# A decoder layer on one core: mixer products in another order, weight tiles in another place, x written later

## The chip, the cores and the metric

The kernel runs on one core of one Trainium2 chip. The metric is the device time of one execution in microseconds (us), and less is better. Before the change the median of three runs is 936.56 us (935.53 to 938.85).

A core has a matrix engine (TensorE, PE in the profile, with its weight loads as PEld), a vector engine (DVE), a scalar engine (ACT), GpSimd (POOL) and a sync engine (SP) that here only issues DMAs. Each engine works through its own queue of instructions in order and waits on semaphores for the others. Matmul results go to PSUM, eight banks of 128 x 512 float32 here; everything else lives in SBUF.

## The reference

One layer on x of 512 tokens by 1024 columns, all in float32: a half-step SwiGLU FFN, a token mixer, another half-step FFN, each between RMS norms.

```python
x = x + 0.5 * rms_norm(swiglu_ffn(rms_norm(x, norm_pre[0]), ffn1_w_in, ffn1_w_out), norm_post[0])
mixed = token_mixer(rms_norm(x, norm_pre[1]), w_mix_in, conv_w, ..., w_mix_out)
x = x + rms_norm(mixed, norm_post[1])
x = x + 0.5 * rms_norm(swiglu_ffn(rms_norm(x, norm_pre[2]), ffn2_w_in, ffn2_w_out), norm_post[2])
```

The mixer projects the normed x with w_mix_in into nine groups of columns. Four of 512 columns feed HGRN2 (query hq, forget hf, value hi, gate hgate), the others an mLSTM (query and key through a causal convolution, value mv, output gate mo, and eight gate rows). Both are recurrences over chunks of tokens.

```python
hg_o = rms_norm(hgrn2_chunkwise(silu(hq), 1 - forget, hi, log(forget))) * silu(hgate)
ml_o = rms_norm(mlstm_chunkwise(q, k, mv, log_i, log_f)) * sigmoid(mo)
mixed = concatenate([hg_o, ml_o]) @ w_mix_out
```

## The kernel before

**Precision.** TensorE multiplies in a rounded float32 form (fp32r). Each operand is split into a rounded part and the rest, and a product takes three matmuls (high by high, high by low, low by high). Weights come by DMA into `raw` tiles; ACT rounds them into the tile `w` (L289), or with a scale per row (L294), and DVE makes the rest (L291, or L297). `split` does both for one item of weights. Activations are split the same way into `xq0` to `xq3`, the four quarters of the transposed x (by half of the tokens and half of the columns): after 128 x 128 transposes on PE (L359), ACT rounds (L365) and DVE makes the rest (L366).

**Where the weight tiles lie.** All `w` tiles are cut out of one long SBUF tile of four places. `lie` chooses a place and an offset in it, from a list for each kind of item: `"any"` prefers offset 0, `"mix"` prefers 16 elements (64 bytes) less, `"out"` 80 elements less. With the offset 0 a tile's address is 480 mod 512 bytes, with -16 it is 416. In `split` a mixer item is of kind "mix" if its tile is 256 (`QUARTER`) or 512 columns wide, except those of w_mix_out that are "out".

**The two units.** The products for hgate ("hg") and mo ("mo"), each 512 tokens by 512 columns by 1024, are made from seven quarter products instead of eight. `job_unit` runs p1 to p7 in the order of `UNIT`; each has 24 matmuls of 256 columns (L1181) on one weight tile and one quarter, or a sum of quarters, of x. Results accumulate in PSUM banks: `bank["b6"]` holds sums into which p6 and then p3 accumulate; p2 runs on top of p1's bank, p4 on top of p5's; p7 has its own. After a product the combinations are made: p1's bank is copied (L1191, ACT), p5 has it subtracted and goes to b6 (L1170, DVE), p6's bank is copied by ACT (L1198) and p7's added by DVE. `put` is called for each finished quarter of the result: for hg an ACT silu (`job_kept`), for mo an ACT sigmoid (L1896) and a DVE multiply into y (L1898), both in `gate_mo`. p3 writes into bank b6 and so waits until p6 has been taken out of it.

**Sums of quarters.** p3, p5, p6 and p7 take differences and sums of x's quarters. `x_sums` queues eight DVE instructions (L1138, 128 x 1024 each), of which four add the two parts of a quarter and four combine them; two casts on ACT and a DVE subtraction each (`sum_parts`, L1161 and L1162) round and split them. They write over the tiles `xs0` to `xs3`, which hold x itself. So x is first written to DRAM, by four DMAs of 512 KB on SP (`spill`, L1839), and read back before the mixer's output is added.

**The order of the work.** The program is emitted once, in order; the queue of an engine is the order in which its instructions were emitted. `self.jobs` holds generators of PE work, and `fill`, `chunks` and `until` take steps of them between the steps of the recurrences; `self.extra` holds small pieces such as the x sums that are taken along. `until(name)` runs jobs until that name is in `self.got`. A planner of due times issues loads and splits ahead of their use. `behind(i)` has what follows scheduled only after the instruction i; `self.loaded` is the last weight load that was issued.

The mixer goes in this order: FFN 1's last tiles, the spills and x sums, the gate weights and forget gates (`hf`), then `hgrn_levels` for the first pair of heads (on DVE and ACT the tiles q, qe, qd, kk, ek, el, with L1478, L1481, L1429, L1439, L1471, L1472; on PE the scores L1490 in pairs of 16 matmuls), filled up with the projections of hq and the convolution (L544), then the second pair, hi and mv, the states, the mLSTM scores, the hg unit, the mLSTM values, the mo unit within the HGRN values. In the HGRN values DVE reduces the squares of a chunk (L1769), POOL makes the power (L350, L351), DVE scales into y (L1775); ACT makes the squares (L1766). After `until("mo")` sixteen transposes of y's HGRN half (`to_t`, L359) lead to `mix_out0`, whose matmuls are L193 to L195 (512 columns wide); it transposes the other half in its second part. At the same time POOL and SP build sums of weight quarters for FFN 2 in DRAM (`f2sums`, accumulating DMAs of POOL at L902).

Of the kernel before, what the change touches and what calls it, by code (L numbers as in the profile page):

```python
# [10 lines left out]
AF = mybir.ActivationFunctionType  # L11
ALU = mybir.AluOpType
# [6 lines left out]
NT = T // P  # L19
# [7 lines left out]
QUARTER = 256  # L27
# [1 line left out]
NH = 4  # L29
W = 512  # L30
HQ, HF, HI, HG, MQ, MV, MO, MG = 0, 512, 1024, 1536, 2048, 2560, 3072, 3584
UNIT = ("p1", "p5", "p7", "p2", "p6", "p4", "p3")
UNITS = (HG, MO)
LEVELS = (1, 64, 32, 16, 8, 4, 2)
TINY = 1e-37
# [85 lines left out]
class Layer:  # L121
# [144 lines left out]
    def split(self):  # L266

        nc = self.nc
        it = self.items.popleft()
        raw = self.raw[it.key]  # L270
        _, a, b = raw.shape
        if it.dst:
            w = it.dst()
        else:
            if self.wt is None:
                self.wt = self.wp.tile([P, 2 * D * WBUF + FRONT + PAD], F32R, name="w")
            if not self.slot and it.key[0] != "mix":
                self.free = deque(FREE2 if it.key[0] == "f2" else FREE)
            n, o = self.lie("out" if it.key[1] == "out" else "mix" if it.key[0] == "mix" and b >= QUARTER else "any")
            self.free.remove(n)  # L280
            w = self.wt[:, o : o + 2 * D].rearrange("p (b k t) -> p b k t", b=2, k=a)
            self.slot[id(w)] = n, o, w
        hi, lo = self.both(w)
        if it.sums:
            raw, hi, lo = (self.flat(v)[:, QUARTER:] for v in (raw, hi, lo))
        self.ready.append((w, it.dst is not None))
        rows = it.rows
        if rows is None:
            nc.scalar.copy(hi, raw)  # L289
            yield  # L290
            self.low = nc.vector.tensor_tensor(lo, raw, hi.bitcast(F32), op=ALU.subtract)  # L291
        else:
            for j in range(a):
                nc.scalar.activation(hi[:, j], raw[:, j], AF.Copy, scale=rows[:, j : j + 1])  # L294
            yield
            for j in range(a):
                nc.vector.scalar_tensor_tensor(  # L297
                    lo[:, j], raw[:, j], rows[:, j : j + 1], hi[:, j].bitcast(F32), op0=ALU.mult, op1=ALU.subtract
                )
        with self.behind(*self.hold):  # L300
            for out, other in it.adds:
                o, c = self.raw[out], self.raw[other]

                late = out[1] >= (HEAD if out[0] == "f1" else 1)
                added = (nc.vector if late else nc.gpsimd).tensor_tensor(o, o, c, op=ALU.add)  # L305
                if not late:
                    self.pooled.append(added)
        self.load_due(self.done)
        self.done += 1
        yield  # L310
# [51 lines left out]
    def two(self, dst, i, src):  # L362

        v = slice((i % 2) * P, (i % 2 + 1) * P)
        self.nc.scalar.copy(dst[:, 0, :, v], src)  # L365
        self.low = self.nc.vector.tensor_tensor(dst[:, 1, :, v], src, dst[:, 0, :, v].bitcast(F32), op=ALU.subtract)  # L366
# [798 lines left out]
    def job_unit(self, name, put, keep):  # L1165

        if name == "hg":
            self.sum_parts("p6", "p3")
        nc, bank = self.nc, {"b6": self.whole}
        tt = lambda out, a, b, op: nc.vector.tensor_tensor(out, a, b, op=op)  # L1170
        two = lambda t: t.rearrange("p (c f) -> p c f", c=2)
        into = {"p2": "p1", "p4": "p5", "p6": "b6", "p3": "b6"}
        for p in UNIT:
            w, x = self.pull(), self.unit_x[p]
            if p not in into:
                bank[p] = self.ps()
            ps, n = bank[into.get(p, p)], 0
            for a, b in ((0, 0), (0, 1), (1, 0)):
                for c in range(2):
                    for k in range(KH):  # L1180
                        nc.tensor.matmul(  # L1181
                            ps[:, QUARTER * c : QUARTER * (c + 1)], x[a][:, k, P * c : P * (c + 1)], w[:, b, k, :],
                            start=p not in into and n == 0, stop=(a, k) == (1, KH - 1), skip_group_check=True,
                        )
                        n += 1
                        if n % 6 == 0 and n < 24:
                            yield
            self.drop(w)
            if p == "p1":
                first = keep(1, 0)  # L1190
                nc.scalar.copy(first, two(ps))  # L1191
            elif p == "p5":
                tt(two(bank["b6"]), two(ps), first, ALU.subtract)
            elif p == "p2":
                put(0, 0, two(ps))
            elif p == "p6":
                rest = keep(1, 1)
                nc.scalar.copy(rest, two(ps))  # L1198
                tt(rest, two(bank["p7"]), rest, ALU.add)
            elif p == "p4":  # L1200
                last = keep(1, 0, two(ps))
                tt(last, two(ps), rest, ALU.subtract)
                put(1, 1, rest)
                put(1, 0, last)
            elif p == "p3":
                put(0, 1, two(ps))
                self.got.add(name)
            yield

    def job_kept(self, name, place, func):  # L1210

        def put(u, v, src):
            if u == 0:
                self.nc.scalar.activation(place(u, v), src, func)
            elif v == 0:
                for v in range(2):
                    self.nc.scalar.activation(place(1, v), place(1, v), func)

        return self.job_unit(name, put, lambda u, v, ps=None: place(u, v))
# [605 lines left out]
    def mixer(self):  # L1825
        nc, tc = self.nc, self.tc
        self.got, self.jobs = set(), deque()
        self.sums_due(("f2",), AHEAD, EARLY["f2"])
        with tc.tile_pool(name="ma", bufs=1) as ma:
# [5 lines left out]
            self.kdt = ma.tile([P, NH, 3 * P], F32, name="kdt")  # L1835
            self.S = self.kdt.rearrange("p h (c v) -> p h c v", v=P)
            self.eend = ma.tile([P, 16], F32, name="eend")
            for i in range(NT):
                nc.sync.dma_start(self.spill[i], self.xs[i])  # L1839
            self.x_sums()  # L1840
            with tc.tile_pool(name="mb", bufs=1) as mb:
                self.mb = mb
                kes = [mb.tile([P, 2, T], F32, name=f"ke{n}") for n in range(2)]
                self.q = [mb.tile([P, 2, T], F32, tag="q", bufs=2, name=f"q{p}") for p in range(2)]
                qps = {}
                for n in range(NH):
                    self.jobs.append(self.job_f(f"hq{n}", lambda ps, n=n: qps.__setitem__(n, ps)))
                for n in range(4):
                    self.jobs.append(self.job_f(f"conv{n}", lambda ps, n=n: self.conv(n, ps)))
                self.jobs.append(self.job_rows())  # L1850
                self.jobs.append(self.job_t("hi", lambda i, ps: nc.scalar.copy(self.vh[:, i].rearrange("p h v -> p (h v)"), ps)))
                self.jobs.append(
                    self.job_t("mv", lambda i, ps: nc.scalar.copy(self.vm[:, i, :, :P], ps.rearrange("p (h v) -> p h v", h=NH)))
                )

                with tc.issue_after(self.pow.ins):
                    self.gate_weights(ma, mb)
                self.forget_gates(mb)
                for ke in kes:
                    nc.scalar.copy(ke, self.kk[0])  # L1860
                with tc.issue_after(self.pow.ins):
                    nc.gpsimd.memset(self.sT, 0.0)
                    self.masks(ma, mb)
                    nc.gpsimd.memset(self.vm[:, :, :, P : P + 1], 1.0)
                self.until("hq3")
                for n in range(NH):
                    nc.scalar.activation(self.q[n // 2][:, n % 2], qps[n], AF.Silu)
                self.hgrn_levels(0, kes, FILL[0])
                self.until("rows")
                nc.scalar.activation(self.qk, self.qk, AF.Silu)  # L1870
                self.hgrn_levels(1, kes, FILL[1], self.gate_rows(ma))
            with tc.tile_pool(name="mc", bufs=1) as mc:
# [7 lines left out]
                self.chunks(self.mlstm_values, FILL[2])  # L1880
                self.until("hg")
                self.chunks(self.hgrn_values, FILL[3])
                self.until("mo")
                for i in range(NT):
                    self.to_t(i, self.y[:, i], (0,))
                self.new_x()
                for i in range(NT):
                    nc.sync.dma_start(self.xs[i], self.spill[i])
# [2 lines left out]
    def keep_mo(self, u, v, ps=None):  # L1891
        return self.st("mo").rearrange("p (c f) -> p c f", c=2) if ps is None else ps

    def gate_mo(self, u, v, g):
        nc = self.nc
        nc.scalar.activation(g, g, AF.Sigmoid)  # L1896
        y = self.y[:, 2 * u : 2 * u + 2, W + QUARTER * v : W + QUARTER * (v + 1)]
        nc.vector.tensor_tensor(y, y, g, op=ALU.mult)  # L1898

# [128 lines left out]
```

## Time and profile before

| | |
|---|---|
| median of three runs | 936.56 us |
| profiled execution | 935.1 us, its span 933.4 |
| granted TensorE clock, mean | 0.997 |
| busy: PE, DVE, ACT, POOL | 919.5, 789.1, 537.7, 215.3 us |
| matmuls | 7567, of which 336 at L1181 |
| DMA | 161.19 MB, queue q1 49.1% and q0 14.7% of 16 engines' span |

The trace is one profiled execution. A line of a timeline gives the start in us from the start of the span, the busy time, engine, line, operation, out<-in, shape and count of a run of like instructions, and in brackets the idle time before it with what ended it. A line of a table of windows gives the length, then the busy time of PE, PEld, DVE, ACT and POOL with counts, the granted TensorE clock, the share of the DMA engines' time and GB/s. A line of the waits gives the waiting engine and line, what it waited for, and the total, the number and the longest of these waits. The busy time of a matmul overlaps that of the next, so what one costs is read from start to start. A waiting time can be read as lost only on the engine that sets the end; that is mostly PE, which is busy 99% of the span.

### The profile page before, as it was taken

The numbers are of one execution on the slowest core, as the hardware profiler recorded it, in microseconds if no ns is written. First come the engines' busy times: TensorE is split into PE (matmuls) and PEld (weight loads), VectorE is DVE, ScalarE is ACT, GpSimd is POOL, SyncE is SP. The second block draws the span as 40 slices with busy tenths as digits, with TensorE's granted clock in tenths as the row PEclk, the third lists the DMA queues.
The fourth block names the chain that finished last, engine by engine and source line by source line (L and its number), as shares of the span: only waits on it lengthen the run. The fifth ranks groups of instructions, "written<-read, shape, count | busy, mean of one in ns | idle before, by whom it ended". The sixth has DMA issues, their size and how long they took to land.

```text
span 933.4 us, 18752 instructions
## 1 busy us (share of the span) xinstructions
PE 919.5 (99%) x7567; PEld 892.1 (96%) x7567; DVE 789.1 (85%) x1016; ACT 537.7 (58%) x773; POOL 215.3 (23%) x280
## 2 busy tenths in 40 slices
PE   9999999999999999999999989999999999999997
PEld 7999999999999999998889978899999999999997
DVE  6899988889887879698868674799898989998886
ACT  7645545557566466956536454595454545756661
POOL 3565112132122047452331310304000000011002
PEclk9999999999999999999999999999999999999999
DMA  9869869887897834797854454452453445278542
GB/s 314 224 161 245 208 176 206 203 181 184 237 265 237 260 131 121 150 183 193 174 115 117 141 173 132 138 159 67 138 159 115 136 122 171 82 218 262 168 153 91
DMA packets 131025, 161.19 MB, mean 173 GB/s; under 512 B 8405, under 2 KB 103673, under 8 KB 130938
## 3 DMA queue, kind: packets, MB, share of 16 engines
q1 hardware_dynamic: 110490, 140.59, 49.1%
q0 software_dynamic: 20160, 18.88, 14.7%
q8 instruction: 59, 0.97, 0.4%
q10 hardware_dynamic: 288, 0.52, 0.2%
q14 instruction: 28, 0.23, 0.1%
HBM read 155.77 MB, written 41.94 MB: 212 GB/s over the span
## 4 chain that ended last, share of the span: by engine, by line
PE 56%; DVE 3%; issue 2%; POOL 1%; ACT 1%; DVEq 0%; POOLq 0%; ACTq 0%
PE ps L615 22%; PE ps L970 8%; PE ps L544 6%; PE ps L962 4%; PE ps L193 3%; PE ps L195 3%; PE ps L194 3%; PE ps L1490 2%; PE ps L1181 2%; PE ps L554 1%; POOL col L351 1%; DVE w L291 1%; PE ps L359 1%; ACT w L294 0%; PE ps L1583 0%
## 5 line engine op out<-in xcount | busy, mean ns | idle before, releaser
L289 ACT CAST w<-raw 128x1024 fp32r<-128x1024 f32 x252 | 257.6, 1028 | 179.3 <-PE ps L615 91.4
L291 DVE TENSOR_TENSOR w<-raw,w 128x1024 fp32r<-128x1024 f32 x252 | 306.3, 1220 | 18.8 <-ACT w L289 17.7
L615 PE MATMUL ps<-xq,w 128*128 128x256 f32 x2016 | 237.2, 277 | 0.0
L615 PEld LDWEIGHTS ps<-xq,w 128*128 128x128 f32 x2016 | 232.9, 188 | 0.0
L615 PE MATMUL ps<-sq,w 128*128 128x256 f32 x1512 | 177.9, 276 | 0.3
L615 PEld LDWEIGHTS ps<-sq,w 128*128 128x128 f32 x1512 | 174.2, 188 | 0.9 <-ACT ps L666 0.9
L305 DVE TENSOR_TENSOR raw<-raw,raw 128x1024 f32<-128x1024 f32 x72 | 89.8, 1251 | 7.9 <-DMA raw<-in_ffn_w_in_dram 6.3
L970 PE MATMUL ps<-w,hs 128*128 128x256 f32 x672 | 81.3, 276 | 0.0
L962 PE MATMUL ps<-w,hs 128*128 128x256 f32 x672 | 79.2, 276 | 0.0
L970 PEld LDWEIGHTS ps<-w,hs 128*128 128x128 f32 x672 | 78.5, 188 | 0.2 <-DVE y L486 0.2
L962 PEld LDWEIGHTS ps<-w,hs 128*128 128x128 f32 x672 | 77.5, 188 | 0.0
L902 POOL DMA_DIRECT2D f2sums<-in_ffn_w_out_dram x15 | 19.5, 1426 | 177.8 <-DMA f2sums<-in_ffn_w_out_dram 176.9
L544 PE MATMUL ps<-xq,w 128*128 128x256 f32 x480 | 55.7, 277 | 0.0
L544 PEld LDWEIGHTS ps<-xq,w 128*128 128x128 f32 x480 | 54.9, 188 | 0.5 <-issue 0.5
L193 PE MATMUL ps<-w,xq 128*128 128x512 f32 x128 | 51.2, 403 | 2.0 <-ACT xq L365 1.9
L194 PE MATMUL ps<-w,xq 128*128 128x512 f32 x128 | 49.9, 391 | 0.0
L195 PE MATMUL ps<-w,xq 128*128 128x512 f32 x128 | 49.6, 391 | 0.1
L834 ACT CAST hs<-hf 128x1024 fp32r<-128x1024 f32 x32 | 33.7, 1053 | 27.5 <-PE ps L970 19.8
L902 POOL DMA_DIRECT2D f2sums<-f2sums x30 | 25.2, 879 | 87.2 <-DMA f2sums<-in_ffn_w_out_dram 50.5
L835 DVE TENSOR_TENSOR hs<-hf,hs 128x1024 fp32r<-128x1024 f32 x32 | 39.1, 1221 | 6.6 <-ACT hs L834 6.1
L305 POOL TENSOR_TENSOR raw<-raw,raw 128x1024 f32<-128x1024 f32 x12 | 31.6, 2640 | 41.0 <-DVE w L291 39.6
L448 ACT ACTIVATE junk<-ps 128x256 f32<-128x256 f32 (+1 forms) x40 | 17.1, 428 | 40.7 <-DVE ps L927 20.1
(287 smaller groups left out, 1355.6 us busy)
## 6 DMA issues: line engine op xcount, KB each, us to landing
raw<-in_ffn_w_in_dram SPq DMA_DIRECT2D x98, 512.0 KB, 4.6
raw<-in_ffn_w_out_dram SPq DMA_DIRECT2D x44, 512.0 KB, 5.5
raw<-in_w_mix_in_dram SPq DMA_DIRECT2D x26, 512.0 KB, 4.1
raw<-f2sums SPq DMA_DIRECT2D x15, 512.0 KB, 3.3
raw<-f1sums SPq DMA_DIRECT2D x13, 512.0 KB, 5.9
raw<-unit SPq DMA_DIRECT2D x8, 512.0 KB, 4.3
raw<-in_w_mix_out_dram SPq DMA_DIRECT2D x8, 512.0 KB, 4.1
f2sums<-in_ffn_w_out_dram SPq DMA_DIRECT2D x30, 128.0 KB, 5.7
```

What stands on the lines that cost most here:

```text
L193: mm(ps, sh, mh, start=start, stop=False, **kw)
L194: mm(ps, sh, ml, start=False, stop=False, **kw)
L195: mm(ps, sl, mh, start=False, stop=stop, **kw)
L289: nc.scalar.copy(hi, raw)
L291: self.low = nc.vector.tensor_tensor(lo, raw, hi.bitcast(F32), op=ALU.subtract)
L305: added = (nc.vector if late else nc.gpsimd).tensor_tensor(o, o, c, op=ALU.add)
L544: mm(ps[:, u0:u1], w[:, a, k, :], self.xop(k, b, u0, u1), start=k + n + m == 0, stop=k == ND - 1 and n == 2, skip_group_check=True,)
L615: self.nc.tensor.matmul(ps[:, c], wb[b][:, k, v], left[d][:, k, :], start=first and a + n + k == 0, stop=n == 2 and k == KH - 1, skip_grou ...
L835: self.nc.vector.tensor_tensor(lo, src, hi.bitcast(F32), op=ALU.subtract)
L902: nc.gpsimd.dma_start(to[:, a:b], v, accum_op=ALU.add)
L962: mm(out, a[kk][:, i * P : (i + 1) * P], w[:, b, kk, QUARTER * v : QUARTER * (v + 1)], start=begin and c == kk == n == 0, stop=kk == 1 and ...
L970: mm(ps[:, QUARTER * c : QUARTER * (c + 1)], A[a][:, c], B[b], start=begin and c == n == 0, stop=n == 2, skip_group_check=True,)
```

## The change

- `UNIT` changes from p1, p5, p7, p2, p6, p4, p3 to p1, p5, p7, p6, p2, p3, p4, and the weights are loaded in that order.
- In `job_unit` ACT copies p7's bank (instead of p6's), as soon as p7 is done, and DVE adds p6's bank to the copy. That quarter is put at once, its sigmoid for mo going into p7's bank (`spare`). p3 comes before p4 and adds the name "mo3" to `got`.
- In the mixer, `until("mo3")` leads to the sixteen transposes, and `until("mo")`, with p4, comes after them.
- In `split` a mixer tile is of kind "mix" only if it is 512 columns wide; the 256-wide ones are "any".
- The four spill DMAs and `x_sums()` move from the start of the mixer to after the forget gates, behind the last load issued there. On DVE the first of the eight adds then stands between two levels of the first pair of heads, after an L291, and the other seven spread over the next 28 instructions; on ACT the two casts L1161 come between the casts and exponentials of the same levels.

On DVE the add of p6's bank in the mo unit stands behind the fourth L1769 of the HGRN values and ahead of two L297 and the fourth chunk's L1775.

```diff
-UNIT = ("p1", "p5", "p7", "p2", "p6", "p4", "p3")
+UNIT = ("p1", "p5", "p7", "p6", "p2", "p3", "p4")
...
-            n, o = self.lie("out" if it.key[1] == "out" else "mix" if it.key[0] == "mix" and b >= QUARTER else "any")
+            n, o = self.lie("out" if it.key[1] == "out" else "mix" if it.key[0] == "mix" and b == 512 else "any")
...
+            elif p == "p7":
+                rest = keep(1, 1)
+                nc.scalar.copy(rest, two(ps))
+            elif p == "p6":
+                tt(rest, two(ps), rest, ALU.add)
+                put(1, 1, rest, two(bank["p7"]))
             elif p == "p2":
                 put(0, 0, two(ps))
-            elif p == "p6":
-                rest = keep(1, 1)
-                nc.scalar.copy(rest, two(ps))
-                tt(rest, two(bank["p7"]), rest, ALU.add)
+            elif p == "p3":
+                put(0, 1, two(ps))
+                self.got.add(name + "3")
             elif p == "p4":
                 last = keep(1, 0, two(ps))
                 tt(last, two(ps), rest, ALU.subtract)
-                put(1, 1, rest)
                 put(1, 0, last)
-            elif p == "p3":
-                put(0, 1, two(ps))
                 self.got.add(name)
             yield
...
-        def put(u, v, src):
+        def put(u, v, src, spare=None):
...
-            for i in range(NT):
-                nc.sync.dma_start(self.spill[i], self.xs[i])
-            self.x_sums()
             with tc.tile_pool(name="mb", bufs=1) as mb:
...
                 self.forget_gates(mb)
+                with self.behind(self.loaded):
+                    for i in range(NT):
+                        nc.sync.dma_start(self.spill[i], self.xs[i])
+                self.x_sums()
                 for ke in kes:
                     nc.scalar.copy(ke, self.kk[0])
...
-                self.until("mo")
+                self.until("mo3")
                 for i in range(NT):
                     self.to_t(i, self.y[:, i], (0,))
+                self.until("mo")
                 self.new_x()
...
-    def gate_mo(self, u, v, g):
-        nc = self.nc
-        nc.scalar.activation(g, g, AF.Sigmoid)
+    def gate_mo(self, u, v, src, spare=None):
+        nc = self.nc
+        g = src if spare is None else spare
+        nc.scalar.activation(g, src, AF.Sigmoid)
         y = self.y[:, 2 * u : 2 * u + 2, W + QUARTER * v : W + QUARTER * (v + 1)]
         nc.vector.tensor_tensor(y, y, g, op=ALU.mult)
```

## The prediction

> **What bounds the kernel now.** I read the busy table of the page first, then the waits of TensorE, then timelines of PE, DVE, ACT and POOL around each edited place.
>
> ```profile
> PE 919.5 (99%) x7567; PEld 892.1 (96%) x7567; DVE 789.1 (85%) x1016; ACT 537.7 (58%) x773; POOL 215.3 (23%) x280
> ```
> ```profile
> PE ps L1181 <- ACT mo L1198: 2.4, 1, 2.4
> PE ps L193 <- ACT xq L365: 1.9, 1, 1.9
> PE ps L189 <- POOL ident masks.py:199: 1.6, 1, 1.6
> PE ps L554 <- DVE w L291: 0.8, 1, 0.8
> PE ps L1181 <- DVE y L1808: 0.2, 1, 0.2
> ```
> TensorE is busy all but 14 us. So an edit can save only a cheaper matmul or one of these waits, of which the first, second and fourth lie where the diff works. The PE timeline shows the first two and something the waits do not count:
>
> ```profile
> 537.48 3.60 PE L1181 MATMUL ps<-w,xq 128*128 128x256 f32 x28
> ...
> 541.88 3.04 PE L1181 MATMUL ps<-w,xq 128*128 128x256 f32 x24
> 547.33 2.74 PE L1181 MATMUL ps<-w,xq 128*128 128x256 f32 x16 [2.41 <-ACT mo L1198]
> 549.87 1.91 PE L1181 MATMUL ps<-w,xpart 128*128 128x256 f32 x8
> 551.57 2.15 PE L359 MATMUL ps<-ident,y 128*128 128x128 f32 x16
> 555.57 0.50 PE L193 MATMUL ps<-w,xq 128*128 128x512 f32 x1 [1.85 <-ACT xq L365]
> ```
> ```profile
> 548.00:552.00 4.00, 4.00 (x24) 4.00 (x23) 4.00 (x9) 1.12 (x2) 0.00 (x0) 0.58 0.15 40
> ```
> p4 (24 matmuls from 541.88) ends at 544.92 and PE idles 2.41 us. p3 then takes 551.57 - 547.33 = 4.24 us, though 24 matmuls at the pace of the first row (3.44 us for 28, 123 ns) are 2.9. The row of 548 to 552 (length, busy time of the five engines, granted clock, DMA share, GB/s) says why: the granted clock is 0.58. The last eight of p3 start (551.57 - 549.87) / 8 = 212 ns apart. So the idle time cost 2.41 us and then over 1 us more at a slow clock; the 1.85 us before L193 had no such sequel.
>
> **Part 1: the place of the weight tiles.** The 256-wide mixer tiles move by 64 bytes. What a matmul costs at each place is read between starts:
>
> ```profile
> 493.16 4.41 PE L1181 MATMUL ps<-w,xpart 128*128 128x256 f32 x36
> 497.50 1.16 PE L1673 MATMUL ps<-qk 64*128 64x128 f32 x16
> ```
> ```profile
> 377.81 10.48 PE L544 MATMUL ps<-xq,w 128*128 128x256 f32 x91
> 388.12 1.95 PE L1536 MATMUL ps<-q,kk 128*128 128x128 f32 x16
> ```
> L1181 runs at 4.34 / 36 = 120.6 ns, L544 of the same width at 10.31 / 91 = 113.3 ns, with its operands at other distances. No row shows L1181 at the new place; bounds are 0 (the place is nothing) and -7.3 ns each, and a like amount above zero if it is worse. I take -7, since a 256-wide matmul is seen at 113 wherever else it runs. Of 336 unit matmuls about 264 get the new place; the hg unit's half gives 132 x 7 = -0.9 us. mo's first five products gain it only to wait longer (part 2); its last two are counted there. The mix_out tiles are 256 wide in the same test, so 48 of their 512-wide matmuls more sit at "any"; I put +4 ns each on them, +0.2, half of what the 256-wide ones differ by. Together **-0.7** (bounds +1.1 and -1.2).
>
> [...]
>
> **Part 2: the end of the mo unit.** Now p6 (into bank b6) is copied out by ACT at L1198, which frees b6 for p3. That copy came late, behind the gates and casts of ACT's queue. The change copies p7 early, adds p6 on DVE straight from b6, and p3 waits for that DVE add. In the new instruction order the add stands on DVE behind the fourth reduction of the HGRN values (L1769), and PE does p2 only, some 2.8 us, between p6 and p3.
>
> ```profile
> 528.71 0.18 DVE L1801 RECIPROCAL col<-col 128x4 f32<-128x4 f32 x1
> ...
> 529.23 1.22 DVE L291 TENSOR_TENSOR w<-raw,w 128x1024 fp32r<-128x1024 f32 x1
> 531.90 0.76 DVE L1808 TENSOR_TENSOR y<-ps,col 128x256 f32<-128x256 f32 x2 [1.45 <-POOL col L1805]
> 532.58 0.69 DVE L1170 TENSOR_TENSOR ps<-ps,mo 128x512 f32<-128x512 f32 x1
> ...
> 534.31 0.68 DVE L1769 TENSOR_REDUCE col<-sq 128x4 f32<-128x512 f32 x1
> ...
> 544.82 0.67 DVE L1769 TENSOR_REDUCE col<-sq 128x4 f32<-128x512 f32 x1
> 546.90 0.61 DVE L1775 SCALAR_TENSOR_TENSOR y<-ps,col,y 128x128 f32<-128x128 f32 x2 [1.41 <-POOL col L351]
> ```
> ```profile
> 529.37 1.13 POOL L350 TENSOR_SCALAR col<-col 128x4 f32<-128x4 f32 x1 [2.34 <-DVE col L1803]
> ...
> 535.07 0.20 POOL L350 TENSOR_SCALAR col<-col 128x4 f32<-128x4 f32 x1 [3.20 <-DVE col L1769]
> ```
> The chain of reductions, POOL powers and scalings is not PE's: it runs 544.82 - 534.31 = 10.5 us from first to fourth whatever PE does. Its start gains some 0.4 us, because L291 now stands ahead of L1802 and POOL's L350 no longer takes 1.13 us beside it but 0.20. So: fourth reduction 544.4, add 545.0 to 545.7, p3 at 545.7. PE, at the end of p6 at 541.88 before, ends p2 at some 541.5 with what part 1 saves, and waits 4.2 us. The wait at L1198 doesn't go; it changes its owner and is longer. The slow clock will come again: I take its price for p3 as before, some 12 matmuls at 212 instead of 120 ns, 1.1 us (bounds 0 and 2).
>
> ```profile
> 567.01 1.36 PE L359 MATMUL ps<-ident,y 128*128 128x128 f32 x11
> ```
> From 545.7: p3 at 113 ns 2.7, slow clock 1.1, 16 transposes at 1.36 / 11 = 124 ns 2.0, p4 2.7: mix_out0 starts at 554.2. L365 and L366, which kept L193 waiting 1.85 us, lie beside p4 now; without that cover they would cost their 1.85 again. 555.57 becomes 554.2: **-1.4**, bounds -2.5 (no slow clock) and -0.1 (2 us for it, and the DVE chain no earlier). In mix_out0 p4's gate comes last instead of p3's, 11 us ahead of its transposes: nothing.
>
> [...]
>
> **Part 3: x written later.** Four spill DMAs and eight DVE adds (L1138) leave the end of FFN 1 for the first HGRN levels.
>
> ```profile
> L1138 DVE TENSOR_TENSOR xsum<-xq x4: 1216/1218/1275, 340.8 to 360.3; 128x1024 f32<-128x1024 f32 x4
> L1138 DVE TENSOR_TENSOR xsum<-xsum,xsum x4: 1218/1237/1273, 356.6 to 365.7; 128x1024 f32<-128x1024 f32 x4
> ```
> The gain: the add at 340.8 delayed the L291 for which L554 waits 0.8 us; without it **-0.7** (0 to -0.84). The price: DVE takes 8 x 1.15 = 9.2 us more between 386 and 421.
>
> ```profile
> 381.13 1.23 DVE L291 TENSOR_TENSOR w<-raw,w 128x1024 fp32r<-128x1024 f32 x1 [2.50 <-ACT w L289]
> ...
> 386.14 1.23 DVE L291 TENSOR_TENSOR w<-raw,w 128x1024 fp32r<-128x1024 f32 x1
> 389.98 0.69 DVE L1478 TENSOR_TENSOR qe<-qe,q 128x512 f32<-128x512 f32 x1 [2.61 <-ACT qe L1473]
> 391.76 1.23 DVE L291 TENSOR_TENSOR w<-raw,w 128x1024 fp32r<-128x1024 f32 x1 [1.09 <-ACT w L289]
> ...
> 400.77 0.55 DVE L1649 TENSOR_SCALAR qk<-cx,prm 128x512 f32<-128x512 f32 x1 [0.92 <-ACT cx L1645]
> ...
> 427.99 1.29 DVE L1478 TENSOR_TENSOR qe<-qe,q 128x512 f32<-128x512 f32 x2
> ```
> ```profile
> 430.94 3.61 PE L1490 MATMUL ps<-qe,ke 128*124 128x64 f32 x32
> ```
> DVE's idle time there is 2.61 + 1.09 + 0.92 = 4.6 us, and it starts some 1.4 us earlier (an estimate: the 0.7 of PE, and as much since DVE and ACT shed x-sum work before 366). So it ends the stretch 9.2 - 6.0 = 3.2 us later. The consumer is L1490: the second half of the 32 matmuls of 430.94, thus from 432.7, needs the qe finished at 429.3, a slack of 3.4, less the 0.7 that PE gains: 2.7. DVE is late by **+0.5** if it never waits for a spill (bounds 0 and, by the rival below, +9). A spill must have landed before its add may overwrite x's place. They leave SP behind the load that the L291 of 381.13 lets go when it ends at 382.4, 1 us earlier now, at about 381.4:
>
> ```profile
> raw<-in_w_mix_in_dram SPq DMA_DIRECT2D x26, 512.0 KB, 4.1
> ...
> spill<-xs SPq DMA_DIRECT2D x4, 512.0 KB, 2.9
> ```
> ```profile
> 383.00:385.00 2.00, 2.00 (x20) 2.00 (x19) 1.89 (x2) 1.97 (x3) 1.96 (x3) 1.00 0.68 171
> ...
> 387.00:389.00 2.00, 2.00 (x20) 2.00 (x19) 0.36 (x1) 1.98 (x3) 1.69 (x2) 1.00 1.15 90
> ```
> DVE reaches the first add at 386.0, the second at 387.2, the fourth at 392.8. Four spills each as long as one alone, one after the other, land from 384.3 to 393.0, in time within 0.5 us. But the last column but one, the DMA share, is 1 from 387 on, with POOL's accumulating DMAs, and later landings are possible; that is the rival below. Moves on SP delay its later loads by some 2 us of issue and transfer, behind weights that are needed over 10 us later: nothing.
>
> **The sum.** -0.7 - 1.4 - 0.7 + 0.5 = -2.3, and -0.2 for mo's first product, ahead of the DVE chain: **-2.5 us**. It is made on the profiled run, 935.1 us, of which 933.4 are span; the median of the runs is 1.5 higher. 936.56 - 2.5 = **934.1 us**. Within 0.3% (2.8 us, above 933.8) is about what a measurement of this kernel can't tell from no change; the forecast stands close to that bound.
>
> **Rivals.**
> - *The clock stays or the add comes early.* If p3's wait brings no slow clock, part 2 is -2.5, and with DVE's idle time taking the adds whole (0 for +0.5) the sum is -4.1: 932.5; with an add that also comes 1.5 us earlier 931.0. For it: 1.85 us of idle left the clock full. Against: 4.2 us is more than the 2.41 that did not.
> - *The change of place does nothing:* what differs between 120.6 and 113.3 ns is then the surroundings, not the address; part 1 and the -0.2 become 0 and the sum -1.6, 935.0. For it: no row holds the place alone apart. [...]
> - *Spills land late, slower.* From 384 POOL's accumulating DMAs take the same 16 engines. If each of the four spills takes 4.3 us instead of 2.9, about what the loads of that size take, the fourth lands at 381.4 + 17.2 = 398.6. The fourth add then begins 5.8 us after 392.8, with all that DVE has to do for L1490 behind it, and PE waits in up to three places. The slack is used up by then, so each us is one of PE: +5.8, and +1.1 for a slow clock where one wait passes 2.4 us. -2.5 + 6.9 = +4.4: 941.0. It decides, past +2.8, from a delay of 4.2 us on (4.2 + 1.1 - 2.5), a fourth landing at 397.0. For it: a DMA share above 1. Against: a load's 4.1 is its time to landing, and several of them overlap.
>
> **Chances.** The forecast case (932.6 to 935.6) 0.39, of it 0.20 below the bound and 0.19 above; the first rival 0.22, faster; the second 0.10, no change; late spills 0.29, of it 0.27 slower and 0.02 no change. Faster 0.42, no change 0.31, slower 0.27. The range from 930.5 to 941.0 takes in the full gain and the late spills up to a fourth landing near 398.6, and leaves about 0.2 out, most of it above. The likeliest case's own range is 932.6 to 935.6.
>
> **What would show it.** L1181 starts 113 to 114 ns apart; PE waits about 4 us at p3 for DVE L1170 and none for L365; the granted clock dips after it; L554's wait is gone; L1490 waits under 1 us on DVE. I am wrong if L1490 or L544 wait for DVE by several us with the adds held by DMA, if L1170 is done before PE reaches p3, or if the spacing of L1181 stays at 120 ns.

## The result, and the profile after

The changed kernel is slower: a median of 939.75 us against 935.77 for the kernel before on the same chips (16 executions each), ratio 1.0034 with a 95% interval of 1.0018 to 1.0050. As one more kernel (c1 below) it gave 1.0020 (1.0007 to 1.0033). I had forecast 934.1 within 930.5 to 941.0, with the larger chance on faster.

The profiled execution took 937.87 us, its span 936.2, against 935.1 and 933.4 before. The waits of TensorE in it (engine and line <- what it waited for: total us, times, longest). L1480, L1492, L1771 and L1810 of the changed kernel are L1478, L1490, L1769 and L1808 of the kernel before:

```profile
PE ps L1181 <- DVE mo L1170: 3.8, 1, 3.8
...
PE ps L1181 <- DVE y L1810: 0.6, 1, 0.6
...
PE ps L970 <- DVE y L486: 0.2, 1, 0.2
PE ps L1492 <- DVE qe L1480: 0.2, 1, 0.2
```

L1198, L365 and L554 are gone from the list, as forecast; in their place p3 waits 3.75 us for DVE's L1170. The PE timeline of the changed kernel around it, and the clock in a table of windows (columns as told above):

```profile
541.22 2.98 PE L1181 MATMUL ps<-w,xq 128*128 128x256 f32 x24
547.96 3.75 PE L1181 MATMUL ps<-w,xq 128*128 128x256 f32 x16 [3.75 <-DVE mo L1170]
551.50 1.86 PE L1181 MATMUL ps<-w,xpart 128*128 128x256 f32 x8
553.21 1.91 PE L359 MATMUL ps<-ident,y 128*128 128x128 f32 x16
554.87 3.07 PE L1181 MATMUL ps<-w,xq 128*128 128x256 f32 x24
557.78 0.40 PE L193 MATMUL ps<-w,xq 128*128 128x512 f32 x1
```
```profile
547.96:551.50 3.54, 3.54 (x16) 3.54 (x17) 3.54 (x9) 2.22 (x4) 0.62 (x1) 0.50 0.36 113
551.50:553.20 1.70, 1.70 (x9) 1.70 (x9) 1.19 (x2) 0.17 (x1) 0.00 (x0) 0.50 0.36 137
```

All of p3 runs at half clock: (553.21 - 547.96) / 24 = 219 ns from start to start. The trace's clock record has the half from 546.36 to 553.19 us, 6.8 us, against 3.4 (548.63 to 552.05) in the kernel before. The place of L1170 is as forecast too; these are DVE's rows:

```profile
546.54 0.68 DVE L1771 TENSOR_REDUCE col<-sq 128x4 f32<-128x512 f32 x1
547.13 0.68 DVE L1170 TENSOR_TENSOR mo<-ps,mo 128x512 f32<-128x512 f32 x1
547.73 1.40 DVE L297 SCALAR_TENSOR_TENSOR w<-raw,prm,w 128x512 fp32r<-128x512 f32 x2
```

Where the 2.8 us of the two spans come from is not in these rows. Setting the n-th matmul of one execution against the n-th of the other, the changed kernel is 0.7 us ahead at 290 us, falls behind from there, by 0.25 us in every 57 matmuls of lines the change does not touch (L970, L962, L544), and is 1.5 us behind at 415 us, though it gains 0.7 us at L554 on the way. It is 2.3 us behind at 526 us, where the mo unit waits 0.6 us for L1810 (0.2 before), 2.2 at the start of mix_out0 and 2.1 at the last matmul; the other 0.7 us of the two spans lie behind that. The slow pace begins behind the wait of L970 in the list above. The windows of that unedited work show it, first of the kernel before, then of the changed one; the number in brackets behind PE's busy time is that of the matmuls:

```profile
300.00:330.00 30.00, 30.00 (x267) 30.00 (x267) 22.75 (x27) 14.57 (x24) 3.28 (x9) 1.00 0.83 255
```
```profile
300.00:330.00 30.00, 30.00 (x257) 30.00 (x256) 21.78 (x26) 14.29 (x24) 2.44 (x8) 1.00 0.78 231
```

Both are fully busy at a granted clock of 1.00, and yet 267 and 257 matmuls fit, 113 and 118 ns apart (start to start). So the profiles alone do not say whether the change is slower, or this execution of it.

### The profile page after: what moved, and what is told of

Its sections match the earlier page's. It is cut to its first block, busy times and chain, and to the rows that moved or that the text cites. A ratio compares the mean times of both kernels' runs of the same rounds, so it can differ in the third digit from the quotient of the medians.

```text
span 936.2 us, 18745 instructions
## 1 busy us (share of the span) xinstructions
PE 922.0 (98%) x7567; PEld 896.5 (96%) x7567; DVE 787.6 (84%) x1016; ACT 534.9 (57%) x771; POOL 209.8 (22%) x280
## 4 chain that ended last, share of the span: by engine, by line
PE 59%; DVE 6%; issue 2%; DMA 1%; ACT 1%; POOL 1%; SPq 0%; DVEq 0%; POOLq 0%; ACTq 0%
PE ps L615 22%; PE ps L970 10%; PE ps L962 7%; PE ps L1181 4%; PE ps L544 3%; PE ps L193 3%; PE ps L195 2%; PE ps L194 2%; DVE w L291 1%; PE ps L1492 1%; DMA spill<-xs 1%; PE ps L359 1%; DVE qk L1654 1%; PE ps L554 1%; PE ps L1764 0%
## 5 line engine op out<-in xcount | busy, mean ns | idle before, releaser
L291 DVE TENSOR_TENSOR w<-raw,w 128x1024 fp32r<-128x1024 f32 x252 | 306.4, 1220 | 25.0 <-ACT w L289 23.8
L970 PE MATMUL ps<-w,hs 128*128 128x256 f32 x672 | 81.9, 277 | 0.2 <-DVE y L486 0.2
L962 PE MATMUL ps<-w,hs 128*128 128x256 f32 x672 | 80.3, 278 | 0.0
L970 PEld LDWEIGHTS ps<-w,hs 128*128 128x128 f32 x672 | 79.0, 188 | 0.4 <-DVE y L486 0.4
L962 PEld LDWEIGHTS ps<-w,hs 128*128 128x128 f32 x672 | 78.6, 188 | 0.0
L544 PE MATMUL ps<-xq,w 128*128 128x256 f32 x480 | 57.5, 282 | 0.0
L544 PEld LDWEIGHTS ps<-xq,w 128*128 128x128 f32 x480 | 56.6, 189 | 0.5 <-issue 0.5
L193 PE MATMUL ps<-w,xq 128*128 128x512 f32 x128 | 51.1, 400 | 0.1
```

The source lines that it names most:

```text
L193: mm(ps, sh, mh, start=start, stop=False, **kw)
L544: mm(ps[:, u0:u1], w[:, a, k, :], self.xop(k, b, u0, u1), start=k + n + m == 0, stop=k == ND - 1 and n == 2, skip_group_check=True,)
L962: mm(out, a[kk][:, i * P : (i + 1) * P], w[:, b, kk, QUARTER * v : QUARTER * (v + 1)], start=begin and c == kk == n == 0, stop=kk == 1 and ...
L970: mm(ps[:, QUARTER * c : QUARTER * (c + 1)], A[a][:, c], B[b], start=begin and c == n == 0, stop=n == 2, skip_group_check=True,)
```

## The experiments

Three theories stood at first. P: the difference is the pace of PE in code that was not edited, an accident of an execution. S: writing x later makes DVE wait for the spills, and PE for DVE. W: p3's wait for L1170, with the slow clock after it, costs more than the covered L365 saves.

**c0, the kernel before again.** No edit.

> The kernel before, unchanged, as one more kernel. Theory P (pace): the profiles of before and after differ by 2.0 us in code that the change does not touch, because between 290 and 400 us a 256-wide matmul starts every 113 ns in the one and every 118 ns in the other; if this is an accident of an execution and not of the change, this run's ratio is 1.000, its single times spread over 4 us (934 to 939), and its profile may show 118 ns in stretches where the first profile shows 113. Theory S (spills) and theory W (the wait at p3) expect the same ratio, with a granted clock of 0.997 in every execution, since no execution has a second slow window.

Ratio 1.0001 (0.9986 to 1.0017). Its twelve times run from 934.47 to 939.52, and in none of the 47 executions of the kernel before on that chip is the granted clock under 0.995. The profile (934.58 us, its span 932.9) has the waits of PE of the first profile within 0.3 us and a span 0.5 us shorter, which leaves no room for a long stretch at 118 ns, some 4 us in 100. So a spread of 5 us at clocks of 0.995 to 0.997 belongs to the unchanged kernel, which fits an accident of pace. That pace makes this spread is only suggested, by the profiles of other kernels (e4 and e8 below).

**e1, x later alone.**

```diff
-            for i in range(NT):
-                nc.sync.dma_start(self.spill[i], self.xs[i])
-            self.x_sums()
...
                 self.forget_gates(mb)
+                with self.behind(self.loaded):
+                    for i in range(NT):
+                        nc.sync.dma_start(self.spill[i], self.xs[i])
+                self.x_sums()
```

> Before with only the spills and the x sums moved to after the forget gates. Theory S: the adds wait on DVE for the spills, in some executions long enough that L1490 waits for qe by more than 2 us and the clock falls; the time is 2 to 4 us above before, with executions of a lower granted clock than before's. Theory P: the wait of L554 goes (-0.7), L1490 waits 0.2 us, the rest is pace: between -1 and +1 us. Theory W: -0.5 us, since the end of the mo unit is as before.

Median 937.95, ratio 1.0026 (1.0011 to 1.0041): slower, about +2.4 us. Four of its twelve executions have a granted clock of 0.992 or 0.993, which the kernel before never has. DVE and PE in its profile:

```profile
387.73 1.23 DVE L1138 TENSOR_TENSOR xsum<-xq 128x1024 f32<-128x1024 f32 x1 [2.06 <-DMA spill<-xs]
389.73 1.23 DVE L1138 TENSOR_TENSOR xsum<-xq 128x1024 f32<-128x1024 f32 x1 [0.77 <-DMA spill<-xs]
...
391.75 1.23 DVE L1138 TENSOR_TENSOR xsum<-xsum,xsum 128x1024 f32<-128x1024 f32 x1 [0.20 <-DMA spill<-xs]
```
```profile
421.68 1.86 PE L1490 MATMUL ps<-qe,ke 128*120 128x64 f32 x16 [1.20 <-DVE qe L1478]
432.05 1.95 PE L1490 MATMUL ps<-qe,ke 128*124 128x64 f32 x16 [0.25 <-ACT ke L1474]
434.37 1.83 PE L1490 MATMUL ps<-qe,ke 128*126 128x64 f32 x15 [0.38 <-DVE qe L1478]
```

DVE waits 3.0 us for spills, and 30 to 45 us later PE waits 1.8 us at L1490 in three places. In this execution the clock stayed full there: the 16 matmuls behind the longest of these waits take 1.86 us, as against 2.87 at half clock in e5 below. The eight executions with a clock of 0.994 or more have a median of 937.4, 1.7 us above the kernel before, the other four 940.2. L554's wait is 0.1 instead of 0.8 us, the gain that was forecast.

**e2, the place of the tiles alone.**

```diff
-            n, o = self.lie("out" if it.key[1] == "out" else "mix" if it.key[0] == "mix" and b >= QUARTER else "any")
+            n, o = self.lie("out" if it.key[1] == "out" else "mix" if it.key[0] == "mix" and b == 512 else "any")
```

> Before with only the 256-wide mixer tiles at the other place. My prediction has -0.9 us for it (113 instead of 120 ns between starts of L1181 in the hg unit, half of mo's gain lost in the wait at p3). Theory P: L1181 goes at 118 ns at either place, the time is within 0.5 us of before. Theories S and W say nothing of it.

Median 935.23, ratio 0.9993 (0.9980 to 1.0005): not to be told from no change, nor from the -0.9 us of my prediction; the rows decide. The run of 36 matmuls of L1181 that I had read the price from:

```profile
492.90 4.54 PE L1181 MATMUL ps<-w,xpart 128*128 128x256 f32 x36
497.37 1.16 PE L1673 MATMUL ps<-qk 64*128 64x128 f32 x16
```

4.47 / 36 = 124 ns at the new place, 120.6 at the old: nothing like 113. This is hardly an accident of an execution: in the changed kernel's profile, with the other order of the products and much of the code before them at 118 instead of 113 ns, the same run starts every 124.1 ns (36 from 495.12 to 499.59 us). Other runs of L1181 go the other way: the 24 of p4 ahead of mix_out0 start 121.3 ns apart in the changed kernel (above) and 123.3 in e3 (below), which has the old place. Over the gaps of the two units (those under 170 ns) the mean is 118.7 ns in the trace of the kernel before and 118.0 in that of the changed one, a gain of some 0.2 us in all.

**e3, the order alone.** The changed kernel with the old place and x early: `UNIT`, the copy of p7's bank with the add of p6, and the transposes after "mo3" are all that differs from before.

> Before with only the order of the products, p7's copy in place of p6's and the transposes ahead of p4. Theory W: p3 waits about 4 us for DVE's L1170, so long that the clock is at half for two windows instead of one in most executions; what is gained by the covered L365 (1.85 us) goes for that, and the time is 0 to 2 us above before, the granted clock 0.994 instead of 0.997. My prediction has -1.4 us. Theory S: -1 us or better, as the loss is in the spills. Theory P: within 1 us of before.

Median 934.67, ratio 0.9984 (0.9971 to 0.9997), -1.5 us by the ratio and -1.0 by the medians; I had forecast -1.4. p3 waits and the clock falls, and in the profiled execution (935.27 us, one of its longer ones) mix_out0 starts when it did before:

```profile
545.46 3.76 PE L1181 MATMUL ps<-w,xq 128*128 128x256 f32 x16 [3.61 <-DVE mo L1170]
549.01 1.91 PE L1181 MATMUL ps<-w,xpart 128*128 128x256 f32 x8
550.72 2.21 PE L359 MATMUL ps<-ident,y 128*128 128x128 f32 x16
552.68 3.12 PE L1181 MATMUL ps<-w,xq 128*128 128x256 f32 x24
555.64 0.40 PE L193 MATMUL ps<-w,xq 128*128 128x512 f32 x1
```

So the wait and the clock of W are there, p3 again at (550.72 - 545.46) / 24 = 219 ns, but the covered L365 pays for them in this profile, and by the times it pays more than that: W, by which this part would cost time, is wrong. Where the gain of the other executions comes from, this profile does not show.

**c1, the changed kernel again.** No edit.

> The changed kernel, unchanged, as one more kernel, to see the ratio again and to have a second profile, in which unedited code between 290 and 400 us may run at 113 ns a matmul. Theory X (x later costs, and with it the clock): the ratio is again 1.003; if the pace is 113, PE comes to L1492 2 us earlier than in the first profile, and waits there for qe not 0.2 but about 2 us. Theory A (the first profile is right, and the cost is the pace): with 113 ns the profiled time falls to 936 and L1492 waits under 0.5 us.

Ratio 1.0020 (1.0007 to 1.0033); its profile (935.97 us, clock 0.997) has 267 matmuls from 300 to 330 us, so 113 ns there, and the slow pace only later: 129 from 360 to 375 us, where the kernel before has 135. With PE earlier, L1492 waits more than in the first profile:

```profile
PE ps L1181 <- DVE mo L1170: 3.7, 1, 3.7
...
PE ps L1492 <- DVE qe L1480: 0.5, 1, 0.5
PE ps L1492 <- ACT ke L1476: 0.3, 1, 0.3
```

0.8 us, between the two theories' numbers, at a profiled time that is theory A's. So one program has either pace in the same stretch; it is an accident of an execution, and the change is slower over many of them. Five of twelve executions have a granted clock of 0.991 to 0.993 and a median of 938.85; the other seven have 936.39.

**e4, the changed kernel with x early.** The spills and x sums back at the start of the mixer.

> The changed kernel with the spills and x sums back at the start of the mixer, so the new order and the new place together. Theory X: the parts add up, -1.5 and -0.6, so 2 us under before, and all of what the change costs is in x later. Theory I (the new order or place costs more in company): within 0.5 us of before or above it.

Median 934.18, ratio 0.9988 (0.9977 to 1.0000), all clocks 0.995 to 0.997: -1.1 us by the ratio, between the two theories, and with this one part undone the slowdown is gone. Its profiled execution (938.48) was the slowest of its twelve by 3 us, and again has 257 matmuls from 300 to 330 us; with x early, so the pace is no part of x later either.

**e5, the changed kernel with the old place.**

> The changed kernel with the 256-wide tiles at the old place: new order and x later. Theory X: +2.4 for x later and -1.5 for the order, +1 us against before, and some 2 us under the changed kernel as measured only if the place costs there what it gains alone. If order and x later together already give +3 or more, the two hinder each other, by a wait at L1492 that grows or by a second slow window; the granted clock then shows it (0.991 as in the slow executions of the changed kernel).

Ratio 1.0019 (1.0009 to 1.0029): the place makes no difference there either that these intervals could tell. Four of eleven executions have a clock of 0.991 to 0.993, the profiled one (939.79 us) among them, and it shows what lies behind that number:

```profile
418.93 1.69 PE L1492 MATMUL ps<-qe,ke 128*112 128x64 f32 x16
421.75 2.87 PE L1492 MATMUL ps<-qe,ke 128*120 128x64 f32 x16 [1.13 <-DVE qe L1480]
```
```profile
421.80:425.00 3.20, 3.20 (x18) 3.10 (x19) 3.20 (x6) 1.17 (x3) 1.99 (x2) 0.59 0.53 47
425.00:429.20 4.20, 4.20 (x11) 3.25 (x10) 4.20 (x7) 2.98 (x4) 0.00 (x0) 0.50 0.94 206
429.20:432.00 2.80, 2.80 (x14) 2.26 (x13) 2.74 (x6) 2.77 (x4) 0.85 (x1) 1.00 1.09 319
```

A wait of 1.13 us among the small matmuls of L1492 (64 wide, on weights of 112 and 120 columns) stands just ahead: from 422.4 to 429.2 the clock is at half. Against the kernel before, matmul by matmul, PE falls another 3.2 us behind in that stretch, three times the wait ahead of it. The wait of 1.20 us at the same place in e1's profile was followed by no such stretch.

**e6, p4 in p3's wait.** The kernel of e4, with p4 ahead of p3 and two of the four groups of transposes between them.

```diff
-UNIT = ("p1", "p5", "p7", "p6", "p2", "p3", "p4")
+UNIT = ("p1", "p5", "p7", "p6", "p2", "p4", "p3")
...
-                self.until("mo3")
-                for i in range(NT):
+                self.until("mo4")
+                for i in range(2):
                     self.to_t(i, self.y[:, i], (0,))
                 self.until("mo")
+                for i in range(2, NT):
+                    self.to_t(i, self.y[:, i], (0,))
```

(In `job_unit` p4 adds "mo4" to `got` and p3 "mo".)

> The kernel of e4 with p4 ahead of p3 and two of the four groups of transposes between them, so that PE has p4 to do while DVE's L1170 is late. Theory W (p3's wait and the slow clock are what the order pays): p3 waits under 1 us, no slow window follows, 2 to 4 us under before; what is next late is L366 on DVE, for which L195 then waits 2 to 4 us. If the wait at p3 was paid by nothing but itself, the gain over e4 is all of its 3.6 us; if DVE bounds this place, it is under 1.

Ratio 0.9989 (0.9978 to 0.9999), no better than e4. p3's wait fell from 3.7 to 0.6 us, and PE was 4 us ahead of the kernel before at 548 us. Then it lost all of it:

```profile
PE ps L193 <- ACT xq L365: 2.6, 1, 2.6
...
PE ps L1181 <- DVE mo L1170: 0.6, 1, 0.6
PE ps L195 <- DVE xq L366: 0.6, 1, 0.6
```

and the clock fell after it:

```profile
555.00:560.00 5.00, 5.00 (x14) 3.92 (x13) 2.24 (x4) 0.34 (x1) 0.00 (x0) 0.55 0.74 258
```

The wait at L193 took only part of the gain, as the kernel before has one of 1.85 us there: at 552.19 against 555.57, PE is still 3.4 us ahead at the first L193, and level with it at 560. ACT's queue tells why L365 was late:

```profile
551.05 0.58 ACT L1902 ACTIVATE ps<-ps 128x512 f32<-128x512 f32 x1 [1.92 <-DVE ps L1170]
551.54 1.08 ACT L365 CAST xq<-ps 128x512 fp32r<-128x512 f32 x2
```

The transposes had been in PSUM since 545, but L365 stood behind p4's sigmoid, which waited for p4's own L1170 on DVE.

**e7, only the adds later.** The kernel before, with the spills where they were and the eight adds held behind a low-part instruction of that place on DVE. (`behind` sets a limit to a scheduler, which otherwise orders the instructions of an engine; the account of the kernel ahead of the prediction, by which the queue is the order of emission, was too simple. What the adds do without the hold, no run here shows.)

```diff
-            self.x_sums()
...
                 self.forget_gates(mb)
+                n, hold = len(self.extra), self.low
+                self.x_sums()
+                for k in range(n, len(self.extra)):
+                    self.extra[k] = self.held_back(hold, self.extra[k])
```

> Before with the eight adds alone held back to the first levels of the first pair of heads (between 382 and 394 us on DVE), while the four spill DMAs stay at the start of the mixer and have long landed. Theory SP (the adds cost because DVE waits for spills): DVE takes its 9.2 us of adds there without a wait, L1490 waits under 1 us, L554's 0.8 us is gone, and the time is between -1 and +0.5 us, not the +2.4 of x late alone. Theory DL (the load on DVE alone costs it): L1490 still waits 1 to 2 us, with slow clocks after it in some executions, and the time is 1.5 to 2.5 us above before.

Ratio 0.9993 (0.9983 to 1.0003), clocks 0.996 to 0.998. PE waits nowhere at L1490, and not at L554 for more than 0.1 us. The same 9 us of adds on DVE cost nothing when they do not wait for a DMA: theory SP. They stand at 379 to 399 us in this profile, the last of them some 16 us earlier than in the changed kernel, so the wait, the later place that comes with it and the traffic of the spills at that time are not separated from one another; the load on DVE alone is ruled out.

**e8 and e9, better than both.** e8 is e6 with the first two groups of transposes after p2 (`until("mo2")`) instead of p4; e9 adds the edit of e7.

> The kernel of e6, with the first two groups of transposes after p2 instead of after p4, so that L365 and L366 of these stand on ACT and DVE ahead of the sigmoid and the multiply of p4, which held them up in e6. If L365's place in ACT's queue is what kept e6 at the time of e4, mix_out0 starts 2 to 4 us earlier, no wait of PE there is over 1 us, the clock doesn't fall (0.998) and the time is 4 to 6 us under before. If DVE's chain of the HGRN values bounds the place whatever the order, it is again 1 us under before.

> The kernel of e8 with the adds held back as in e7. Theory SP: L554's wait goes without a new one at L1492: 0.5 to 1 us under e8. Theory DL: 1.5 to 2.5 us above e8.

e8: median 928.82, ratio 0.9935 (0.9916 to 0.9953), 6.1 us under the kernel before by the ratio, at the far end of the 4 to 6 that were expected. e9: median 928.02, ratio 0.9918 (0.9906 to 0.9930), 7.7 us under it; that e9 is faster than e8 is within their intervals. The clock of e9 is 0.998 or 0.999 in all executions. PE in e9:

```profile
541.57 1.03 PE L359 MATMUL ps<-ident,y 128*128 128x128 f32 x8
542.36 3.07 PE L1181 MATMUL ps<-w,xq 128*128 128x256 f32 x24
546.03 2.12 PE L1181 MATMUL ps<-w,xq 128*128 128x256 f32 x16 [0.59 <-DVE mo L1170]
547.99 1.11 PE L1181 MATMUL ps<-w,xpart 128*128 128x256 f32 x8
548.93 1.04 PE L359 MATMUL ps<-ident,y 128*128 128x128 f32 x8
549.72 0.47 PE L193 MATMUL ps<-w,xq 128*128 128x512 f32 x1
```

mix_out0 starts at 549.7, where it started at 555.6 before; p3 takes (548.93 - 546.03) / 24 = 121 ns a matmul, at full clock. e8's profiled execution took 934.17 us, its other five 928.44 to 929.46; in it PE waited 1.1 us at 290 us (L970 for DVE's L486) and then had 257 matmuls from 300 to 330 us. mix_out0 starts at 553.95 us there, 4.2 us later than in e9: 1.6 of them are longer waits (1.1 at L970 and 1.0 at L554, against 0.5 and none), and the other 2.6 fit the pace, as from 360 to 375 us e8 has 130 matmuls and e9 135. What the other five did at that time is not recorded. The wait does not make the pace: e9's profile (929.12) waited 0.5 us there, has 257 as well and ended its slow pace by 360 us, but e1's waited 1.0 us there and shows no such loss (PE is free for the 17th matmul of L1490's 32 there at 420.5 us, and it starts at 421.0 in the kernel before), and e4's has 257 without such a wait. What sets the pace stays open.

## Why the prediction was wrong

- **Part 1, the place (-0.7): wrong in its mechanism.** I read 120.6 against 113.3 ns as a matter of address, with 113 to be had at the other place. The run of 36 takes 124.1 ns there, p4 gains 2 ns a matmul, and the sum of both units is a gain of some 0.2 us. Nor does a 256-wide matmul go at 113 ns "wherever else it runs": in the profile before, 24 of L554 start (355.48 - 352.66) / 24 = 117.5 ns apart. So the address counts for a few ns in either direction, which add up to almost nothing; what keeps L1181 from 113, which the prediction had named as a sign of being wrong, stays open. The rival by which the place is worth nothing, at 0.10, agrees with the sum; the two rows, 120.6 and 124.1 ns, differ all the same.
- **Part 2, the mo unit (-1.4): right in its waits and their order, with one term too small.** e3 measured -1.0 to -1.5. The wait for L1170 (forecast 4.2 us, measured 3.6 to 3.8), its place behind the fourth reduction, the slow clock and the cover of L365 came as worked out. The slow clock, forecast at 1.1 us, cost all 24 matmuls of p3 in the first profile and in e3's, (219 - 120) x 24 = 2.4 us, and 1.3 in c1's, where p3 takes 175 ns a matmul. In e3's profile PE gains nothing on the kernel before between 520 and 570 us, so that the -1.4 meets e3's median is in part luck.
- **Part 3, L554 (-0.7): right.** Its wait went from 0.8 us to 0.1 or nothing.
- **Part 3, the price (+0.5): the step that failed.** "Four spills each as long as one alone, one after the other, land from 384.3 to 393.0, in time within 0.5 us" left out the 512 KB load just ahead of them. In the trace of the changed kernel the load is issued at 381.5 us and the first spill at 381.9, but the spill's data move only from 384.9 on, when nearly all of the load's have gone. The four land at 386.9, 389.6, 391.8 and 393.2 (the last semaphore of each), where the forecast had 384.3, 387.2, 390.1 and 393.0: the fourth in time, the first two 2.5 us late. POOL's DMAs, on queue q0, had no part in the first of these: from 382 to 388 us only the queue of the loads and spills, and one fetch of instructions, move anything (packets, MB, share of 16 engines):

```profile
q1 hardware_dynamic: 600, 1.74, 87.7%
q8 instruction: 1, 0.02, 1.0%
```

  DVE waited at three of the adds, 2.4 us in all:

```profile
386.96 1.23 DVE L1138 TENSOR_TENSOR xsum<-xq 128x1024 f32<-128x1024 f32 x1 [0.51 <-DMA spill<-xs]
389.65 1.23 DVE L1138 TENSOR_TENSOR xsum<-xq 128x1024 f32<-128x1024 f32 x1 [1.46 <-DMA spill<-xs]
...
391.89 1.23 DVE L1138 TENSOR_TENSOR xsum<-xsum,xsum 128x1024 f32<-128x1024 f32 x1 [0.42 <-DMA spill<-xs]
```

  With the adds on it DVE has no idle time left after that, so PE waits at L1490: 0.2 us in this profile, where PE comes late by its pace, and 0.8, 1.1 and 1.8 in those of c1, e5 and e1. And I had the clock fall only from 2.4 us of idle on, whereas in e5 it fell after 1.13 us, for 3.2 us more. Executions with a clock of 0.993 or less occur only in the kernels with x later (4 of 12 in e1, 5 of 12 in c1, 4 of 11 in e5, 7 of 16 in the first measurement), and in none of 168 executions of the kernel before and of the other variants. x later alone is thus +2.4 us, where part 3 as a whole had -0.2.
- **The rival.** "Spills land late, slower", at 0.29, had the direction and the place of the waits, but not the cause: it let each spill take 4.3 us beside POOL's DMAs and decided only from a fourth landing at 397, and the fourth landed at 393.2. It was the first three that were late, with DVE waiting 2.4 us, and the clock made up the rest.
- **The sum.** The parts measured alone, 1.0026, 0.9993 and 0.9984, add to 1.0003, each with some 0.0013 to either side. The changed kernel had 1.0020 and 1.0034. The first lies within what these intervals leave, the second just beyond; whether the two slow-clock stretches together cost more than each alone stays open.

## What to carry to other kernels

A wait on the engine that bounds a kernel costs its length and can cost the clock behind it (1.13 us of wait and then 3.2 more in e5, 1.20 us and no more in e1): look in the windows behind each idle stretch before pricing it, and fill the wait with independent work, but follow the queues of the engines that hand over the result, since the gain of e6 came only when L365 no longer stood behind a sigmoid that waited. A DMA moved later must be priced with whatever stands ahead of it on its queue, and work that overwrites its source inherits its landing, the first one above all (386.9 us instead of 384.3 here). Before a few ns per instruction in one profile are laid to an edit, compare the pace of unedited code between two executions of the same program.

## What the hardware showed that I had not expected

- PE showed two paces at a granted clock of 1.00: a 256-wide matmul of unedited lines starts every 113 or every 118 ns, for tens of us to over 100 us at a time (290 to 408 us in the changed kernel's first profile), 267 or 257 matmuls in 30 us. It is worth some 3 us in that profile, and 2.6 between those of e8 and e9.
- The place of a weight tile shows in single runs of matmuls, 120.6 ns in the kernel before against 124 in e2 and in the changed kernel for the same 36, with hardly any effect on the sum (some 0.2 us).
- The clock fell to half for 6.8 us after a wait of 1.13 us among matmuls of 64 columns (e5), while 1.85 us before mix_out0 left it full in the kernel before, and 1.20 us at the same place in e1. So the idle time alone does not decide. Nor does it set the length alone: at half clock the kernel before spent 3.4 us after the wait of 2.41 us at p3, the changed kernel 6.8 us, which began within its wait of 3.75 us there, and e5 6.8 us after 1.13 us. What sets the fall and its length stays open.
